# Background steps that start at granule 12 of a feed-forward layer, and two GpSimd splits in place of six

## The chip, the cores and the metric

The kernel runs on one core of one Trainium2 chip. The metric is the device time of one execution, in microseconds (us), as the median of several runs. The engines are named as the profile names them: PE is TensorE, DVE is VectorE, ACT is ScalarE, POOL is GpSimd, and SP is SyncE, whose queue issues nearly all weight loads.

## The reference, cut to what matters

Two blocks are computed on one sequence of 256 rows of 1024 numbers. The first has two layers; each is a feed-forward layer (FFN1), a token mixer, a gated projection (ple) and a second feed-forward layer (FFN2), with a layer norm after FFN1, after the mixer and after FFN2. The second block is a hybrid mixer and a mixture of experts. Its inputs are modulated by a vector that hangs on `c` alone and not on the sequence:

```python
def swiglu(x, w_up, w_down):
    a, b = jnp.split(x @ w_up, 2, axis=-1)
    return (jax.nn.silu(a) * b) @ w_down

# first block, for i in range(2)
x = layer_norm(ALPHA * x + 0.5 * swiglu(x, ffn1_up[i], ffn1_down[i]), ln1_g[i], ln1_b[i])
mix = token_mix(x, ...)
x = layer_norm(ALPHA * x + mix, ln2_g[i], ln2_b[i])
ple = jax.nn.sigmoid(x @ w_ple_gate[i]) * (p[i] @ w_ple[i])
x = layer_norm(ALPHA * x + 0.5 * swiglu(x, ffn2_up[i], ffn2_down[i]) + ple, ln3_g[i], ln3_b[i])

# second block
cond = jax.nn.silu(c)
mod = cond @ w_ada[layer] + b_ada[layer]          # 1024 -> 6144
sh_m, sc_m, g_m, sh_f, sc_f, g_f = jnp.split(mod, 6, axis=-1)
```

All is float32. `D_FF` is 2816, so the up matrix has 5632 columns.

## The kernel before, in words

**Matmuls of split numbers.** A float32 weight matrix is loaded in granules of 128 x 1024 numbers (512 KB, `raw`). `load_split` (L227) takes each granule: SP issues the load (L237), ACT writes the rounded high part (`whi`, L161), and DVE or POOL writes the rest (`wlo`, L165). `products` (L211) then makes three matmuls from each pair: high by high (L223), low by high (L224), high by low (L225). A granule is worth 12 matmuls of 512 columns, six for each half `t` of the sequence. There are four `raw` buffers, seven pairs of `whi` and `wlo`, and four pairs more in a pool that lives for one feed-forward layer.

**A feed-forward layer** (`ffn`, L312 before the change) runs over six chunks of the up matrix, five of 512 columns and one of 256, each with an `a` part and a `b` part: 44 granules. Then come the 22 granules of the down matrix. In the first chunk `gemms` (L197) does all eight granules for t=0 and then all eight for t=1, so PE wants a new granule after every six matmuls; in the later chunks it does both halves of a granule in turn. The tuples `pl1` and `pl2` name the granules of the first chunk's `a` and `b` part whose `wlo` is made on POOL: (2, 3) and (0, 1, 2, 3) before. They count for FFN2 of the first layer and both feed-forward layers of the second. `done_b` has DVE multiply `th` by the `b` part (L329) and PE transpose the product (`tp`, L251), which becomes `hh` and `hl`, the input of the down part. The down part ends with its last eight granules for t=0, then the layer norm of t=0 on DVE (L284 to L293) while PE does the same granules for t=1, then the layer norm of t=1; each norm ends with PE transposing `x` (L251) for what follows.

**Background work.** The modulation needs no result of the sequence, and is done in pieces during the feed-forward layers: rows 0 to 3 of the twelve rows of 512 numbers in FFN1 of the first layer (after a list of other constants), rows 4 to 7 in FFN2 of the first layer, rows 8 to 11 in FFN1 of the second. `ada` is a generator; a row has eight steps, each a load of 256 KB (`araw`, two buffers, L833) and a DVE instruction that adds it into `acc` (L842). A finished row is split, summed by two PE matmuls with ones (L820, L821) and written to memory. `load_split` calls `background(1)` once per granule, which runs the generator to its next `yield`. Before, every second step yields twice, so 32 steps take 48 granules.

**What sets the order.** The program is written in the order of the calls, and a scheduler then orders each engine's instructions by priority and by when their inputs come free. An instruction may so be put far ahead of the place where it was written. `pin` (L111) keeps an instruction in program order. Each engine works through its queue strictly in order, and SP too.

Of the kernel before, what the change touches and what calls it, by code (L numbers as in the profile page):

```python
# [14 lines left out]
OP = mybir.AluOpType  # L15
# [56 lines left out]
class Kernel:  # L72
    def __init__(self, tc, a, out, dbg=None):
        self.tc, self.nc, self.a, self.out, self.dbg = tc, tc.nc, a, out, dbg
        self.n = 0
        self.nraw, self.nhl, self.next, self.xp = 4, 7, 4, None
        self.npj, self.ngt, self.glag = 4, 4, 1
        self.dtail = 8
        self.xg = 4
        self.sp, self.late = None, False  # L80
        self.pre, self.npre = [], 5
        self.start = False
        self.na, self.nb = 8, 9
        self.pl1, self.pl2 = (2, 3), (0, 1, 2, 3)
        self.bg = iter(())
        self.scr = {"s4": (1024, 8), "s2": (512, 6)}


# [216 lines left out]
        self.xp = None  # L305

    def background(self, n):
        for _ in range(n):
            next(self.bg, None)

# [499 lines left out]
    def ada(self, r0, r1):  # L810

        nc = self.nc
        w, b = self.a["w_ada_2"][0], self.a["b_ada_2"][0]
        with self.tc.tile_pool(name=self.nm("ada"), bufs=1, side="right") as pool:
            def finish(i, acc):
                hl = self.st(self.wp, [P, 1024], "whi", F32R, bufs=self.nhl)
                hi, lo = hl[:, :512], hl[:, 512:]
                self.split_from(acc, hi, lo)
                pb = self.ps("tp")
                nc.tensor.matmul(pb, self.ones, hi, start=True, stop=False)  # L820
                nc.tensor.matmul(pb, self.ones, lo, start=False, stop=True)  # L821
                nc.scalar.activation(acc[0:1, :], pb[0:1, :], AF.Copy, bias=1.0 if i // 2 in (1, 4) else 0.0)
                nc.gpsimd.dma_start(self.mod[i // 2:i // 2 + 1, (i % 2) * 512:(i % 2) * 512 + 512], acc[0:1, :])

            def start(i):
                acc = self.st(pool, [P, 512], "acc", bufs=2)
                nc.vector.memset(acc, 0.0)
                nc.sync.dma_start(acc[0:1, :], b[i * 512:(i + 1) * 512].rearrange("(o n) -> o n", o=1))
                return acc

            def load(j):
                raw = self.st(pool, [P, 512], "araw", bufs=2)
                nc.sync.dma_start(raw, self.wsrc(w, j % KD, 1, j // KD * 512, 512)[:, 0, :])  # L833
                return raw

            nxt, last, ahead = start(r0), None, load(r0 * KD)
            for i in range(r0, r1):
                acc = nxt
                for k in range(KD):
                    raw, j = ahead, i * KD + k + 1  # L840
                    ahead = load(j) if j < r1 * KD else None
                    nc.vector.scalar_tensor_tensor(acc, raw, self.cond[:, k:k + 1], acc, op0=OP.mult, op1=OP.add)  # L842
                    if k == 3 and last:
                        finish(*last)
                    if k == 5 and i < r1 - 1:
                        nxt = start(i + 1)
                    yield
                    if j % 2:
                        yield
                last = i, acc  # L850
            yield
            finish(*last)
# [980 lines left out]
    def run(self):  # L1833
        nc, a, tc = self.nc, self.a, self.tc
        with tc.tile_pool(name="const", bufs=1) as self.cp, tc.tile_pool(name="small", bufs=2) as self.smp, \
# [23 lines left out]
            with tc.tile_pool(name="ln", bufs=1) as self.lnp:  # L1859
                pl, self.pl1, self.pl2 = (self.pl1, self.pl2), (), ()  # L1860
                for L in range(2):
                    ln = a["ln1_g"][L], a["ln1_b"][L]
                    if L:
                        self.pl1, self.pl2 = pl
                    if L:
                        self.bg = self.ada(8, 12)
                    self.ffn(a["ffn1_up"][L], a["ffn1_down"][L], ln)
                    self.background(999)
                    if self.stop(f"ln1_{L}"):
                        return  # L1870
                    ln = a["ln2_g"][L], a["ln2_b"][L]
                    self.token_mix(L, ln)
                    if self.stop(f"ln2_{L}"):
                        return
                    self.ple(L)
                    self.pl1, self.pl2 = pl
                    ln = a["ln3_g"][L], a["ln3_b"][L]
                    if L == 0:
                        self.bg = self.ada(4, 8)
                    else:  # L1880
                        self.mods = ctx.enter_context(tc.tile_pool(name="mods", bufs=1, side="right"))
                        A, sh = self.mod_pair(self.mods, 0, a["norm_mix_2"][0])
                    self.ffn(a["ffn2_up"][L], a["ffn2_down"][L], ln, last=(load_first, norm_first) if L else None)
                    self.background(999)
                    if self.stop(f"ln3_{L}"):
                        return
# [49 lines left out]
```

## Time and profile before

| what | us |
| --- | --- |
| median of 3 runs | 2527.62 (2524.69 to 2527.79) |
| the profiled execution, whole | 2525.59 |
| its span, first to last instruction | 2524.0 |
| PE busy in the span | 2389.5 (95%) |
| DVE busy | 1313.9 (52%) |
| ACT busy | 827.1 (33%) |
| POOL busy | 209.1 (8%) |

The first block takes about 1310 us. In it FFN1 of the first layer lies at 0 to 216, its FFN2 at about 464 to 671, FFN1 of the second layer at 671 to 872, and its FFN2 at about 1117 to 1310. What follows 1330 us (the mixture of experts, above all) is bound by weight loads, and no line of the change stands in it. In the rows, the number after a `x` counts instructions, a bracket says how long the engine was idle before the first of them, and the name behind `<-` in the bracket is what ended the idle time.

### The profile page before, as it was taken

To read this page: it belongs to the slowest core of one execution; us is meant where nothing else is said; L and a number is where in the kernel's file an instruction comes from. 1 tells how busy PE (TensorE), PEld (TensorE's weight loads), DVE (VectorE), ACT (ScalarE), POOL (GpSimd) and SP (SyncE) were. 2 spreads that over 40 slices of the span, in tenths; PEclk is the share of its full clock that TensorE was granted. 3 is DMA by queue.
4 is the path that set the end of the run, shared out by engine and by line. 5 is a ranking of instruction groups with operands and counts; after the bars stand their busy time and mean duration, and the time that the engine had idled before them with its cause. 6 is when DMAs were issued, how large, how long until landed. Compare 5 with 4: busy or idle time off the path is not lost.

```text
span 2524.0 us, 29376 instructions
## 1 busy us (share of the span) xinstructions
PE 2389.5 (95%) x11078; PEld 1562.4 (62%) x11078; DVE 1313.9 (52%) x2243; ACT 827.1 (33%) x1227; POOL 209.1 (8%) x191
## 2 busy tenths in 40 slices
PE   8998999999799999999988999999999999999998
PEld 6887787778678878878877877433333333333332
DVE  7768757666666676675566775322222222222222
ACT  5443544444345454444435753100000001000000
POOL 4000211200200011230013010000000000000000
PEclk9999999999899999999998999999999999999999
DMA  8777465567666656566547467999999999999997
GB/s 272 242 236 233 144 188 182 184 215 222 210 188 215 217 159 175 171 197 195 184 131 232 118 199 289 399 421 421 420 421 421 420 421 420 420 421 421 421 421 325
DMA packets 202027, 705.94 MB, mean 280 GB/s; under 512 B 18122, under 2 KB 31642, under 8 KB 152984
## 3 DMA queue, kind: packets, MB, share of 16 engines
q1 hardware_dynamic: 194584, 684.02, 74.1%
q0 software_dynamic: 7296, 19.99, 2.7%
q8 instruction: 89, 1.46, 0.2%
q14 instruction: 58, 0.48, 0.1%
HBM read 702.83 MB, written 3.47 MB: 280 GB/s over the span
## 4 chain that ended last, share of the span: by engine, by line
PE 53%; DMA 31%; DVE 9%; issue 3%; ACT 3%; POOL 1%; SPq 0%; ACTq 0%; DVEq 0%; POOLq 0%
DMA mraw<-in_w_dram 25%; PE mm L225 12%; PE mm L224 12%; PE mm L223 12%; PE mm L1590 5%; PE sc L1621 4%; PE tp L251 3%; DVE wlo L165 2%; DMA araw<-in_w_ada_dram 2%; DMA raw<-in_ffn_up_dram 2%; ACT whi L161 1%; DMA raw<-in_w_in_dram 1%; PE tp L1700 1%; PE sc L1519 1%; DVE x L292 1%
## 5 line engine op out<-in xcount | busy, mean ns | idle before, releaser
L165 DVE TENSOR_TENSOR wlo<-raw,whi 128x1024 fp32r<-128x1024 f32 (+1 forms) x451 | 559.0, 1246 | 277.2 <-ACT whi L161 274.5
L161 ACT ACTIVATE whi<-raw 128x1024 fp32r<-128x1024 f32 x478 | 500.7, 1055 | 521.5 <-PE mm L225 386.3
L224 PE MATMUL mm<-wlo,xTh 128*128 128x512 f32 (+2 forms) x1520 | 580.4, 382 | 10.6 <-POOL wlo L165 8.6
L223 PE MATMUL mm<-whi,xTh 128*128 128x512 f32 (+2 forms) x1520 | 585.8, 386 | 2.1 <-ACT whi L161 1.7
L225 PE MATMUL mm<-whi,xTl 128*128 128x512 f32 (+2 forms) x1520 | 579.8, 382 | 0.0
L1590 PE MATMUL mm<-mraw,xe 128*64 128x512 f32 x1920 | 488.5, 613 | 33.6 <-DMA mraw<-in_w_dram 33.5
L1590 PEld LDWEIGHTS mm<-mraw,xe 128*64 128x64 f32 x1920 | 150.6, 141 | 332.6 <-issue 265.2
L224 PEld LDWEIGHTS mm<-wlo,xTh 128*128 128x128 f32 x1520 | 288.6, 190 | 69.8 <-POOL wlo L165 11.5
L223 PEld LDWEIGHTS mm<-whi,xTh 128*128 128x128 f32 x1520 | 289.0, 190 | 56.2 <-ACT whi L161 3.0
L225 PEld LDWEIGHTS mm<-whi,xTl 128*128 128x128 f32 x1520 | 288.6, 190 | 50.0
L1601 ACT ACTIVATE mt<-mg 128x256 f32<-128x256 f32 x64 | 26.6, 416 | 691.5 <-DVE mg L1600 689.5
L1621 PE MATMUL sc<-mraw,xTl 128*64 128x512 f32 x976 | 231.5, 597 | 7.4 <-ACT xe L1530 7.4
L1600 DVE TENSOR_SCALAR mg<-mm 128x256 f32<-128x256 f32 x64 | 27.2, 424 | 323.4 <-PE mm L1590 319.0
L1621 PEld LDWEIGHTS sc<-mraw,xTl 128*64 128x64 f32 x976 | 69.1, 137 | 125.6 <-issue 108.9
L225 PE MATMUL mm<-whi,hl 128*128 128x512 f32 x352 | 138.1, 392 | 0.0
L223 PE MATMUL mm<-whi,hh 128*128 128x512 f32 x352 | 137.6, 391 | 0.0
L224 PE MATMUL mm<-wlo,hh 128*128 128x512 f32 x352 | 137.5, 391 | 0.0
L1626 DVE TENSOR_TENSOR xTh<-sc,gf 128x512 f32<-128x512 f32 x32 | 22.1, 692 | 208.4 <-PE sc L1621 208.4
L1701 DVE TENSOR_TENSOR x<-x,tp 128x512 f32<-128x512 f32 x68 | 46.8, 688 | 129.8 <-PE tp L1700 129.8
L842 DVE SCALAR_TENSOR_TENSOR acc<-araw,cond,acc 128x512 f32<-128x512 f32 x96 | 72.8, 758 | 54.2 <-DMA araw<-in_w_ada_dram 51.8
L165 POOL TENSOR_TENSOR wlo<-raw,whi 128x1024 fp32r<-128x1024 f32 x27 | 68.9, 2564 | 285.6 <-ACT whi L161 285.5
L225 PEld LDWEIGHTS mm<-whi,hl 128*128 128x128 f32 x352 | 66.4, 189 | 13.6
(445 smaller groups left out, 2277.5 us busy)
## 6 DMA issues: line engine op xcount, KB each, us to landing
mraw<-in_w_dram SPq DMA_DIRECT2D x360, 1024.0 KB, 19.8
raw<-in_ffn_up_dram SPq DMA_DIRECT2D x176, 512.0 KB, 4.4
raw<-in_w_in_dram SPq DMA_DIRECT2D x142, 512.0 KB, 4.4
raw<-in_ffn_down_dram SPq DMA_DIRECT2D x88, 512.0 KB, 4.0
araw<-in_w_ada_dram SPq DMA_DIRECT2D x96, 256.0 KB, 3.6
AS<-in_w_dram SPq DMA_DIRECT2D x22, 1024.0 KB
raw<-in_w_branch_dram SPq DMA_DIRECT2D x28, 512.0 KB, 3.9
raw<-in_w_out_dram SPq DMA_DIRECT2D x16, 512.0 KB, 3.7
```

Of the source, the lines that this page charges most:

```text
L161: ins = self.nc.scalar.activation(hi, src, AF.Copy)
L165: ins = (self.nc.gpsimd if pool else self.nc.vector).tensor_tensor(lo, src, hi, op=OP.subtract)
L223: nc.tensor.matmul(banks[b], xh, hi[:, s], start=kc == 0, stop=False)
L224: nc.tensor.matmul(banks[b], xh, lo[:, s], start=False, stop=False)
L225: nc.tensor.matmul(banks[b], xl, hi[:, s], start=False, stop=kc == nk - 1)
L251: self.nc.tensor.transpose(pt[:s.shape[-1], i * P:i * P + s.shape[0]], s, self.ident)
L842: nc.vector.scalar_tensor_tensor(acc, raw, self.cond[:, k:k + 1], acc, op0=OP.mult, op1=OP.add)
L1590: self.pe(nc.tensor.matmul(ph[nb][e * 64:e * 64 + 64], xe[:, k, e * 64:e * 64 + 64], units[e][k][:, nb * 512:nb * 512 + 512], start=False, ...
L1600: nc.vector.tensor_scalar(g, pv[:, :, 0], 7.0, None, op0=OP.min)
L1601: nc.scalar.activation(th, g, AF.Tanh, scale=0.851)
L1621: self.pe(self.nc.tensor.matmul(py[c][e * 64:e * 64 + 64], aT[:, k:k + 64], units[e][j][:, o:o + 512], start=j == 0 and r == 0, stop=j == ...
L1701: nc.vector.tensor_tensor(self.x[t][:, s], self.x[t][:, s], po, op=OP.add)
```

## The change

Four things are done at once.

1. A counter `hold` is set to 12 when the generators for rows 4 to 7 and 8 to 11 are set up. The first twelve calls of `background(1)` of that layer only count it down.
2. The double `yield` goes, so there is one step per granule, and one `yield` comes after a generator's first loads. A generator of 32 steps takes 34 granules: 12 to 45 of the 66 in the two layers with `hold`, and 34 in place of 49 behind the constants in the first.
3. The first DVE step of each generator is pinned to its place in the program.
4. `pl1`, `pl2` become (), (1, 3): two `wlo` of the first chunk on POOL in place of six, in three feed-forward layers. DVE has 12 instructions more in all and POOL 12 fewer.

```diff
-        self.pl1, self.pl2 = (2, 3), (0, 1, 2, 3)
-        self.bg = iter(())
+        self.pl1, self.pl2 = (), (1, 3)
+        self.bg, self.hold = iter(()), 0
...
     def background(self, n):
+        if n == 1 and self.hold:
+            self.hold -= 1
+            return
         for _ in range(n):
             next(self.bg, None)
...
             nxt, last, ahead = start(r0), None, load(r0 * KD)
+            yield
             for i in range(r0, r1):
...
-                    nc.vector.scalar_tensor_tensor(acc, raw, self.cond[:, k:k + 1], acc, op0=OP.mult, op1=OP.add)
+                    ins = nc.vector.scalar_tensor_tensor(acc, raw, self.cond[:, k:k + 1], acc, op0=OP.mult, op1=OP.add)
+                    if (i, k) == (r0, 0):
+                        self.pin(ins)
...
                     yield
-                    if j % 2:
-                        yield
...
-                        self.bg = self.ada(8, 12)
+                        self.bg, self.hold = self.ada(8, 12), 12
...
-                        self.bg = self.ada(4, 8)
+                        self.bg, self.hold = self.ada(4, 8), 12
```

**The layer norm that ends FFN2 of the first layer, on DVE** (`x_71` is half t=0; `wlo_57..` are splits for the coming FFN1; L842 is a step of the modulation). Before:

```order
L165 TENSOR_TENSOR wlo_5350<-raw_5347,whi_5349 128x1024
L165 TENSOR_TENSOR wlo_5722<-raw_5719,whi_5721 128x1024
L284 SCALAR_TENSOR_TENSOR x_71<-mm_5353,x_71 128x512
L285 BN_STATS bn_1201_5573<-x_71 128x6
L842 SCALAR_TENSOR_TENSOR acc_5925<-araw_6014,cond,acc_5925 128x512
L842 SCALAR_TENSOR_TENSOR acc_5925<-araw_6029,cond,acc_5925 128x512
L284 SCALAR_TENSOR_TENSOR x_71<-mm_5354,x_71 128x512
L842 SCALAR_TENSOR_TENSOR acc_5925<-araw_6038,cond,acc_5925 128x512
L285 BN_STATS bn_1201_5573<-x_71 128x6
L842 SCALAR_TENSOR_TENSOR acc_5925<-araw_6123,cond,acc_5925 128x512
L287 BN_AGGR mv_1202_5578<-bn_1201_5573 128x2
```

And with the change:

```order
L165 TENSOR_TENSOR wlo_5728<-raw_5725,whi_5727 128x1024
L165 TENSOR_TENSOR wlo_5734<-raw_5731,whi_5733 128x1024
L284 SCALAR_TENSOR_TENSOR x_71<-mm_5353,x_71 128x512
L285 BN_STATS bn_1201_5573<-x_71 128x6
L284 SCALAR_TENSOR_TENSOR x_71<-mm_5354,x_71 128x512
L285 BN_STATS bn_1201_5573<-x_71 128x6
L287 BN_AGGR mv_1202_5578<-bn_1201_5573 128x2
```

Sixteen steps of rows 8 to 11 stood in and before this norm, ahead of the layer that they were written in, seven of them from its first L285 on; now none does. The same holds for rows 4 to 7 and the norm that ends FFN1 of the first layer.

**The norm of t=1 (`x_72`) behind it, on DVE, with the change.** The splits that have left POOL, and the first `th` of FFN1, stand inside the chain of the norm:

```order
L285 BN_STATS bn_1212_5664<-x_72 128x6 x2
L165 TENSOR_TENSOR wlo_5748<-raw_5745,whi_5747 128x1024
L287 BN_AGGR mv_1213_5669<-bn_1212_5664 128x2
L165 TENSOR_TENSOR wlo_5760<-raw_5757,whi_5759 128x1024
L142 TENSOR_SCALAR rv_1214_5671<-mv_1213_5669 128x1
L292 SCALAR_TENSOR_TENSOR x_72<-x_72,mv_1213_5669,lng_5207 128x512
...
L328 SCALAR_TENSOR_TENSOR th_5795<-th_5795,mm_5743 128x512
...
L165 TENSOR_TENSOR wlo_5896<-raw_5893,whi_5895 128x1024
L156 SCALAR_TENSOR_TENSOR ry_1216_5675<-rt_1218_5679,ry_1216_5675 128x1
L293 SCALAR_TENSOR_TENSOR x_72<-x_72,ry_1216_5675,lnb_5208 128x512 x2
```

On PE, 42 matmuls of FFN1's t=0 half now stand between the end of the down part and the transposes of `x_72`.

**The start of FFN2 of the first layer, on DVE** (L788, L789 before and L791, L792 after are the end of ple). Before, and with the change:

```order
L165 TENSOR_TENSOR wlo_4064<-raw_4061,whi_4063 128x1024
L788 SCALAR_TENSOR_TENSOR pg_3990<-pg_3990,pe_844_3882 128x512
L789 SCALAR_TENSOR_TENSOR x_71<-pg_3990,x_71 128x512
L165 TENSOR_TENSOR wlo_4081<-raw_4078,whi_4080 128x1024
L788 SCALAR_TENSOR_TENSOR pg_4018<-pg_4018,pe_838_3860 128x512
L789 SCALAR_TENSOR_TENSOR x_72<-pg_4018,x_72 128x512
L788 SCALAR_TENSOR_TENSOR pg_4046<-pg_4046,pe_845_3884 128x512
L789 SCALAR_TENSOR_TENSOR x_72<-pg_4046,x_72 128x512
L325 SCALAR_TENSOR_TENSOR th_4160<-th_4160,mm_4102 128x512
```

```order
L165 TENSOR_TENSOR wlo_4070<-raw_4067,whi_4069 128x1024
L791 SCALAR_TENSOR_TENSOR pg_4018<-pg_4018,pe_838_3860 128x512
L165 TENSOR_TENSOR wlo_4076<-raw_4073,whi_4075 128x1024
L792 SCALAR_TENSOR_TENSOR x_72<-pg_4018,x_72 128x512
L165 TENSOR_TENSOR wlo_4082<-raw_4079,whi_4081 128x1024
L791 SCALAR_TENSOR_TENSOR pg_4046<-pg_4046,pe_845_3884 128x512
L792 SCALAR_TENSOR_TENSOR x_72<-pg_4046,x_72 128x512
L165 TENSOR_TENSOR wlo_4090<-raw_4087,whi_4089 128x1024
L165 TENSOR_TENSOR wlo_4102<-raw_4099,whi_4101 128x1024
L328 SCALAR_TENSOR_TENSOR th_4137<-th_4137,mm_4085 128x512
```

DVE takes the splits of `a` 2, `a` 3, `b` 0 and `b` 2 between the steps of ple; POOL keeps `b` 1 and `b` 3.

## Rows read from the trace of the kernel before

**Rows 1.** The page: busy time of the engines in the whole span

```profile
PE 2389.5 (95%) x11078; PEld 1562.4 (62%) x11078; DVE 1313.9 (52%) x2243; ACT 827.1 (33%) x1227; POOL 209.1 (8%) x191
```

**Rows 2.** Who PE waited for, whole span: us in total, times, longest

```profile
PE tp L251 <- DVE x L293: 25.0, 7, 8.1
PE tp L251 <- DVE th L329: 5.6, 4, 3.0
```

**Rows 3.** Busy time by stretch: length, PE PEld DVE ACT POOL, clock, DMA

```profile
147.60:272.39 124.79, 116.88 (x526) 94.32 (x525) 91.80 (x173) 54.77 (x79) 7.82 (x11) 0.96 0.70 220
810.29:924.94 114.65, 113.26 (x525) 91.90 (x524) 75.93 (x146) 53.50 (x77) 8.26 (x12) 1.00 0.61 194
600.05:671.49 71.44, 63.32 (x279) 51.99 (x278) 45.13 (x62) 26.50 (x29) 6.76 (x5) 0.95 0.69 222
810.29:872.41 62.12, 61.90 (x278) 50.75 (x278) 36.58 (x48) 26.97 (x30) 3.96 (x7) 1.00 0.68 222
671.49:693.57 22.08, 15.73 (x62) 12.69 (x61) 18.76 (x26) 7.77 (x10) 10.50 (x6) 0.85 0.64 198
```

**Rows 4.** Timeline of PE: the transposes of x at three norms

```profile
216.64 1.94 PE L251 MATMUL tp<-ident,x 128*128 128x128 f32 x8 [7.21 <-DVE x L293]
665.95 1.09 PE L251 MATMUL tp<-ident,x 128*128 128x128 f32 x4 [8.12 <-DVE x L293]
683.89 1.09 PE L251 MATMUL tp<-ident,x 128*128 128x128 f32 x4 [6.35 <-DVE x L293]
```

**Rows 5.** Timeline of DVE, inside the norm of t=0 at 654 us

```profile
653.79 2.60 DVE L842 SCALAR_TENSOR_TENSOR acc<-araw,cond,acc 128x512 f32<-128x512 f32 x2 [7.09 <-DMA araw<-in_w_ada_dram]
```

**Rows 6.** Who PE waited for at 465:485 us; the answer for 1120:1135 reads alike

```profile
PE mm L224 <- POOL wlo L165: 3.9, 3, 1.6
```

**Rows 7.** Timeline of POOL, DVE and ACT at the start of FFN2, first layer

```profile
461.20 8.20 POOL L165 TENSOR_TENSOR wlo<-raw,whi 128x1024 fp32r<-128x1024 f32 x3 [13.88 <-ACT whi L161]
459.11 0.69 DVE L789 SCALAR_TENSOR_TENSOR x<-pg,x 128x512 f32<-128x512 f32 x1
461.57 2.77 DVE L789 SCALAR_TENSOR_TENSOR x<-pg,x 128x512 f32<-128x512 f32 x1
474.40 2.52 DVE L165 TENSOR_TENSOR wlo<-raw,whi 128x1024 fp32r<-128x1024 f32 x1 [0.26 <-ACT whi L161]
478.35 1.87 DVE L165 TENSOR_TENSOR wlo<-raw,whi 128x1024 fp32r<-128x1024 f32 x1 [1.43 <-ACT whi L161]
469.98 2.95 ACT L161 ACTIVATE whi<-raw 128x1024 fp32r<-128x1024 f32 x3 [3.42 <-DVE x L789]
```

**Rows 8.** Timeline of PE, two matmuls that follow each other at 476 us

```profile
476.46 0.39 PE L223 MATMUL mm<-whi,xTh 128*128 128x512 f32 x1
476.69 0.40 PE L224 MATMUL mm<-wlo,xTh 128*128 128x512 f32 x1
```

**Rows 9.** Timeline of DVE, the undisturbed norm of t=1, first and last piece

```profile
872.46 1.28 DVE L284 SCALAR_TENSOR_TENSOR x<-mm,x 128x512 f32<-128x512 f32 x2
...
878.25 1.42 DVE L293 SCALAR_TENSOR_TENSOR x<-x,ry,lnb 128x512 f32<-128x512 f32 x2
```

**Rows 10.** Timeline of PE: transposes of th that came late

```profile
44.61 0.66 PE L251 MATMUL tp<-ident,th 128*128 128x128 f32 x4 [1.13 <-DVE th L329]
540.60 0.66 PE L251 MATMUL tp<-ident,th 128*128 128x128 f32 x4 [3.00 <-DVE th L329]
750.84 0.66 PE L251 MATMUL tp<-ident,th 128*128 128x128 f32 x4 [1.33 <-DVE th L329]
```

**Rows 11.** Timeline of DVE, the step ahead of the second of these

```profile
539.19 0.75 DVE L842 SCALAR_TENSOR_TENSOR acc<-araw,cond,acc 128x512 f32<-128x512 f32 x1 [4.67 <-DMA araw<-in_w_ada_dram]
```

**Rows 12.** One chunk of FFN2, first layer: length, DVE busy, clock, DMA, GB/s

```profile
565.17:587.92 22.75, 17.12 (x21) 1.00 0.72 222
```

**Rows 13.** Groups of DVE instructions in that chunk: busy, mean ns, idle before

```profile
L165 DVE TENSOR_TENSOR wlo<-raw,whi 128x1024 fp32r<-128x1024 f32 x7 | 8.5, 1220 | 2.1 <-ACT whi L161 2.1
L842 DVE SCALAR_TENSOR_TENSOR acc<-araw,cond,acc 128x512 f32<-128x512 f32 x7 | 5.2, 748 | 3.3 <-DMA araw<-in_w_ada_dram 3.3
```

## The prediction

> **What bounds the kernel now.** I read the page first. PE is busy 95% of the span and no other engine over 52% [rows 1], so time can come only from PE's idle stretches and from stretches in which PE's clock is granted at half. The list of PE's waits names them: 25.0 us behind the last step of a layer norm (`x`, L293), 5.6 us behind `th` of a chunk (L329) [rows 2], and twice 3.9 us behind splits on POOL at the start of the two FFN2 [rows 6]. What lies after 1330 us waits for weights and is not touched by the change, so a microsecond saved before it should be a microsecond at the end.
>
> Then I compare stretches that do the same work. From the first down matmul of FFN1 to the same transposes in the mixer takes 124.79 us in the first layer and 114.65 in the second, the first two of [rows 3], with 526 and 525 PE instructions. From the first down matmul of FFN2, first layer, to the first matmul of the next layer takes 71.44 us, against 62.12 for the same part of FFN1, second layer, the next two of [rows 3], with 279 and 278. In the slower of each pair PE waits 7.21 and 8.12 us for a norm [rows 4], and the granted clock is 0.96 and 0.95 against 1.00. Why the norm is late is seen on DVE: there stands a modulation step that idles the engine for 7.09 us until its load lands [rows 5], with the norm queued behind it.
>
> **The change part by part.** The sum is made against the profiled execution, 2525.59 us; the median of the runs shown is 2.0 us above it.
>
> *Steps out of the norm that ends FFN1, first layer.* The pinned first step keeps all of rows 4 to 7 in FFN2. DVE's order there becomes that of the second layer, which has its own measurement: 124.79 - 114.65 = **10.1 us** gained. The two retired PE sums of a finished row move elsewhere in the same program and cost the same.
>
> *Steps out of the norm that ends FFN2, first layer.* Likewise, 71.44 - 62.12 = **9.3 us**.
>
> *Start of both FFN2, POOL's six splits become two.* PE uses up a granule every six matmuls, 6 x 0.23 = 1.4 us [rows 8]. POOL takes 8.20 / 3 = 2.7 us for a split, DVE 1.22 [rows 7, 13]. Six on POOL are 16 us for eight granules that PE wants within 11; that is the 3.9 us [rows 6]. Now POOL has two (5.4 us) and DVE six (7.3 us), side by side, both under 11. DVE also gets its other work back faster: L789 takes 0.69 us alone and 2.77 while POOL splits, and three `whi` on ACT wait 3.42 us for it [rows 7]. Bounds: nothing, if the splits now wait on DVE as long as they did on POOL, and the whole 3.9. I take the whole, as DVE's row is below PE's pace: 2 x 3.9 = **7.8 us**.
>
> *Start of FFN1, second layer.* Here PE waits 6.35 us for the norm of t=1 [rows 4], in a stretch at clock 0.85, the last of [rows 3]. Undisturbed, the chain from the first L284 to the first half of L293 takes 878.25 + 0.7 - 872.46 = 6.5 us [rows 9]. The change puts three splits (3 x 1.22 = 3.7) and a `th` (0.7) into it: 10.9. Two of the splits meet POOL's two; such a split took 2.52 and 1.87 in place of 1.22 [rows 7], together 2.0 more: 12.9. PE now has 42 matmuls to do meanwhile, 42 x 0.23 = 9.7. It would still wait 12.9 - 9.7 = 3.2 us in place of 6.35, a gain of **3.2 us**. I count nothing for the clock.
> By the Trainium skill (SBUF — State Buffer, section "Who interferes with whom") a DVE instruction with two SBUF inputs and a GpSimd instruction that reads SBUF exclude each other, and whoever is late waits for the whole of the other. By that rule each split could wait a whole POOL split of 2.7 us, the chain would be 6.5 + 3.7 + 0.7 + 5.4 = 16.3 us, and nothing would be gained here; the rows (a delay of 1.3 and 0.65) are of splits that came when POOL's was partly done. With no meeting at all, the chain is 10.9 and the gain 5.2. So 0 and 5 are the ends.
>
> *Steps into the up parts.* Before, 64 of the 96 steps ran in up or down parts without harming a norm, and PE lost 1.13 + 3.00 + 1.33 = 5.5 us to them [rows 10]: a `th` came late because a step ahead of it waited for its load, 4.67 us in the worst case [rows 11]. Now 96 steps run there. At the same rate they cost 5.5 x 96 / 64 = 8.2 us, **2.7 us** more. Is there room on DVE? A chunk of the changed order has eight steps and eight splits. The chunk at 565 us had seven and seven, was 17.12 us busy of 22.75, waited 3.3 us for loads [rows 12, 13], and PE had no idle row in it. With one more of each, 17.1 + 0.75 + 1.22 = 19.1 us, which leaves 3.6 us for waits where 3.3 were seen. It fits, just. Bounds: all the loss goes (5.5 gained), or each chunk loses 3.0 (below).
>
> *The loads.* SP's queue has the modulation's loads in other places, none new. Two `araw` and two `acc` loads per generator still go early, in the down part of the layer before; two buffers are all there are, so no more can, and no step on DVE waits behind them there. The 14.6 us of splits that DVE takes from POOL (12 x 1.22) are counted above, where they stand; elsewhere DVE's idle time covers them.
>
> Sum: 10.1 + 9.3 + 7.8 + 3.2 - 2.7 = 27.7 us. 2525.59 - 27.7 = 2497.9 for an execution like the profiled one, and 2499.9 by the median. I forecast **2499 us**.
>
> **The rivals.**
>
> *A: DVE and its loads become the bound of the up parts, and the kernel is slower.* Some twelve chunks (four in each of three layers) now carry steps at nearly every granule, and SP must fetch each `araw` between weight loads, with two buffers. If in each chunk one load lands as late as the one at 539 us and PE waits 3.0 us behind it [rows 10, 11], that is 36 us, 30.5 more than now, which eats up all the other terms (30.4): 2525.7. At the 4.67 us that DVE waited, 56 us, 50.5 more: 2545.7. It decides from 3.0 us per chunk on. For it: only 3.6 us are free in a chunk. Against it: with seven steps a chunk ran without a PE gap, and the mean loss before was 5.5 us over nine chunks, 0.6 each. Chance 0.07.
>
> *B: splits on DVE are as late as on POOL.* Then the starts give nothing: 10.1 + 9.3 - 2.7 = 16.7, 2508.9. If moreover PE waits for each of the 12 moved splits, 14.6 us go: 2523.5. For it: DVE has ple and the norm to do at these places. Against it: 1.22 against PE's 1.4 us. The Trainium skill (Perfetto Trace Analysis, section "Optimizing Scalar/DVE Operations") says that offloading to GpSimd may make sense where DVE is saturated; by that the change goes the wrong way here, though the same sentence warns of the shared port. Chance 0.15.
>
> *C: the steps still run ahead.* If the pin held the first step only in name, the norms would stay late and only 7.8 + 3.2 = 11.0 be gained: 2514.6. The order of the changed program speaks against it. Chance 0.03.
>
> *D: more goes.* The second norm's wait vanishes whole (6.35) and the up parts lose nothing: 10.1 + 9.3 + 7.8 + 6.4 + 5.5 = 39.1: 2486.5. Chance 0.12.
>
> **How the numbers follow.** 0.63 is left for the forecast, whose own range is 2492 to 2507. The range reaches from a little below D to just beyond C, 2485 to 2516, and leaves out A and the costly end of B. A measurement of this kernel can tell some 0.2%, 5 us, from no change. Slower is A but for its lower end, 0.06; within 0.2% are that end and the costly end of B, 0.03; faster is the rest, 0.91.
>
> **What would show it.** PE's waits behind L293 at the norms of FFN1 and FFN2, first layer, should be under 1 us, and the stretches of the first two pairs read about 115 and 62 us, at clock 1.00. PE's waits for POOL at the two FFN2 should be gone, with L789's successor at 0.7 us. At the start of FFN1, second layer, a wait of about 3 us should stay. PE's waits behind `th` should sum to some 8 us; 30 or more would mean A. DVE should show 12 more splits of 128x1024 and POOL 12 fewer. The prediction is wrong if the norms stay late although no step stands in them, or if DVE waits for `araw` longer than the 3.6 us that a chunk leaves free.

## The result, and the profile after

The changed kernel takes **2501.13 us** (median of 4 runs, 2499.63 to 2504.71), against 2527.51 us for the kernel before on the same chip (4 runs, 2524.69 to 2527.79): a ratio of 0.990, 95% interval 0.9887 to 0.9914. The forecast was 2499 us, and the range 2485 to 2516. The profiled execution took 2501.3 us, its span 2499.5, 24.5 less than the span before. Line numbers of the changed kernel are three or four higher from `background` on: L332 is the old L329, L792 the old L789, L836 the old L833, L846 the old L842.

The page of the changed kernel, busy time of the engines:

```profile
PE 2385.3 (95%) x11078; PEld 1560.2 (62%) x11078; DVE 1311.6 (52%) x2255; ACT 828.2 (33%) x1227; POOL 178.6 (7%) x179
```

DVE has 12 instructions more and POOL 12 fewer [rows 1]. PE does the same work; the gain is in what it waits for and in its clock. Who PE waited for, whole span (total, times, longest):

```profile
PE tp L251 <- DVE th L332: 11.7, 9, 3.4
PE tp L251 <- DVE x L293: 5.8, 6, 2.1
...
PE mm L224 <- POOL wlo L165: 1.9, 1, 1.9
```

The 25.0 us behind `x` [rows 2] have become 5.8, and the 3.9 us at each FFN2 start [rows 6] are gone from those stretches. The 5.6 us behind `th` have doubled. The same by stretch, changed kernel; the first three lines answer to the first, third and last of [rows 3], the last two are the up parts of FFN2 (first layer) and FFN1 (second layer), from the first transposes of `th` to the first down matmul:

```profile
150.88:265.04 114.16, 113.11 (x525) 92.01 (x524) 77.27 (x148) 54.14 (x77) 7.16 (x10) 1.00 0.63 194
592.22:654.28 62.06, 61.92 (x278) 50.86 (x278) 36.24 (x48) 27.87 (x30) 2.03 (x3) 1.00 0.61 195
654.28:669.96 15.68, 13.57 (x65) 10.99 (x64) 15.50 (x28) 7.01 (x9) 5.29 (x4) 1.00 0.66 213
471.15:592.22 121.07, 116.87 (x570) 97.94 (x571) 90.05 (x109) 54.85 (x67) 1.51 (x3) 0.99 0.75 238
669.96:792.16 122.20, 117.94 (x570) 98.66 (x569) 89.77 (x109) 54.85 (x67) 2.66 (x5) 0.97 0.74 235
```

The two up parts in the kernel before:

```profile
481.60:600.06 118.46, 115.46 (x573) 96.69 (x571) 79.67 (x93) 55.31 (x67) 1.51 (x3) 1.00 0.68 215
693.57:810.29 116.72, 115.39 (x573) 96.68 (x571) 78.64 (x92) 55.33 (x67) 2.67 (x5) 1.00 0.66 205
```

The norm stretches now read 114.16 and 62.06, within 0.5 us of their counterparts in the second layer, at clock 1.00. The up parts have sixteen DVE instructions more each (x109 for x93 and x92): they are the steps that stood in the norms. They are 2.6 and 5.5 us longer. In these two layers, and in FFN2 of the second, the first transposes of `th` come three matmuls later than before (x570 for x573), so 0.7 us of work counts in the start that was counted in the up part; their sum is not touched by it.

**The start of FFN1, second layer.** DVE's timeline in the changed kernel, from the first L284 of the t=1 norm to its L293:

```profile
653.80 1.37 DVE L284 SCALAR_TENSOR_TENSOR x<-mm,x 128x512 f32<-128x512 f32 x2 [2.32 <-PE mm L225]
...
656.28 3.25 DVE L165 TENSOR_TENSOR wlo<-raw,whi 128x1024 fp32r<-128x1024 f32 x1
...
659.57 1.17 DVE L165 TENSOR_TENSOR wlo<-raw,whi 128x1024 fp32r<-128x1024 f32 x1
...
665.18 1.41 DVE L293 SCALAR_TENSOR_TENSOR x<-x,ry,lnb 128x512 f32<-128x512 f32 x2
```

POOL's two splits at that time, and PE's transposes of `x` behind the norm:

```profile
653.68 4.77 POOL L165 TENSOR_TENSOR wlo<-raw,whi 128x1024 fp32r<-128x1024 f32 x2 [53.35 <-ACT whi L161]
```

```profile
666.08 0.63 PE L251 MATMUL tp<-ident,x 128*128 128x128 f32 x4 [2.11 <-DVE x L293]
```

One DVE split takes 3.25 us where the next takes 1.17; it stands beside POOL's second split. The chain is 665.18 + 0.7 - 653.80 = 12.1 us, and PE waits 2.11 us in place of 6.35 [rows 4].

**How a `th` comes late.** The longest wait of the changed kernel, 3.37 us at 706 us, in the second layer's FFN1. DVE:

```profile
698.54 0.75 DVE L846 SCALAR_TENSOR_TENSOR acc<-araw,cond,acc 128x512 f32<-128x512 f32 x1 [0.22 <-DMA araw<-in_w_ada_dram]
...
703.60 0.75 DVE L846 SCALAR_TENSOR_TENSOR acc<-araw,cond,acc 128x512 f32<-128x512 f32 x1 [1.38 <-DMA araw<-in_w_ada_dram]
704.27 1.22 DVE L165 TENSOR_TENSOR wlo<-raw,whi 128x1024 fp32r<-128x1024 f32 x1
705.41 1.27 DVE L332 TENSOR_TENSOR th<-th,mm 128x512 f32<-128x512 f32 x2
```

SP, which issues the loads, and then PE:

```profile
699.32 0.33 SPq L836 DMA_DIRECT2D araw<-in_w_ada_dram  x1
```

```profile
706.14 1.12 PE L251 MATMUL tp<-ident,th 128*128 128x128 f32 x4 [3.37 <-DVE th L332]
...
709.62 0.63 PE L223 MATMUL mm<-whi,xTh 128*128 128x512 f32 x1
710.05 0.63 PE L224 MATMUL mm<-wlo,xTh 128*128 128x512 f32 x1
```

With two `araw` buffers a load can go out only when the step two before it has read its buffer: the step of 698.54 ends at 699.29 and SP issues at 699.32. The step that needs the load runs at 703.60, after DVE has idled 1.38 us; a split and `th` are queued behind it, and PE behind `th`. The cost does not end there. After the wait PE's matmuls follow each other at 0.43 us in place of 0.23 [rows 8], and the granted clock says why (changed kernel, 708 to 712 us):

```profile
708.00:712.00 4.00, 4.00 (x12) 3.23 (x11) 3.18 (x5) 0.60 (x1) 0.00 (x0) 0.50 0.85 279
```

PE is busy without a gap there, at the lower of its two levels, 1.2 GHz. The length of a wait does not tell by itself whether the clock falls behind it. Behind a wait of 2.6 us at 507 us it was 0.66, behind the 2.11 us wait at 666 us it stayed at 1.00 (both in the changed kernel), and so it did behind the wait of 3.00 us in the kernel before [rows 10]:

```profile
508.00:512.00 4.00, 4.00 (x14) 3.30 (x14) 3.27 (x5) 0.85 (x3) 0.00 (x0) 0.66 1.02 379
668.00:672.00 4.00, 4.00 (x21) 3.31 (x20) 3.59 (x5) 2.70 (x5) 0.00 (x0) 1.00 0.88 267
540.60:544.00 3.40, 3.40 (x19) 2.70 (x20) 3.40 (x5) 1.20 (x2) 0.00 (x0) 1.00 0.55 146
```

**Where the steps stand.** The chunk whose `th` is 3.37 us late (from the transposes of `th` at 680.8 to those at 706.1) holds ten steps on DVE, and so does the same chunk of FFN2, first layer (482.2 to 506.7), whose `th` is 2.6 us late; the three chunks that follow in each layer hold four, five and eight. What DVE waited for loads in these two, FFN2 first:

```profile
DVE acc L846 <- DMA araw<-in_w_ada_dram: 7.0, 6, 1.8
DVE acc L846 <- DMA araw<-in_w_ada_dram: 7.7, 7, 2.0
```

The prediction named waits of more than 3.6 us in a chunk as a sign that it is wrong; here that sign came.

### The profile page after: what moved, and what is told of

Read it like the earlier page. It is cut to its first block, busy times and chain, and to the rows that moved or that the text cites. A ratio compares the mean times of both kernels' runs of the same rounds, so it can differ in the third digit from the quotient of the medians.

```text
span 2499.5 us, 29387 instructions
## 1 busy us (share of the span) xinstructions
PE 2385.3 (95%) x11078; PEld 1560.2 (62%) x11078; DVE 1311.6 (52%) x2255; ACT 828.2 (33%) x1227; POOL 178.6 (7%) x179
## 4 chain that ended last, share of the span: by engine, by line
PE 41%; DMA 33%; DVE 8%; issue 3%; ACT 2%; POOL 0%; SPq 0%; DVEq 0%; ACTq 0%; POOLq 0%
DMA mraw<-in_w_dram 28%; PE mm L224 10%; PE mm L225 10%; PE mm L223 10%; PE mm L1594 4%; PE sc L1625 3%; DMA araw<-in_w_ada_dram 3%; DVE wlo L165 2%; PE tp L251 2%; ACT whi L161 1%; PE tp L1704 1%; DMA raw<-in_ffn_up_dram 1%; DVE acc L846 1%; DMA raw<-in_w_in_dram 0%; DMA acc<-in_b_ada_dram 0%
## 5 line engine op out<-in xcount | busy, mean ns | idle before, releaser
L165 DVE TENSOR_TENSOR wlo<-raw,whi 128x1024 fp32r<-128x1024 f32 (+1 forms) x463 | 575.1, 1249 | 271.2 <-ACT whi L161 269.3
L1630 DVE TENSOR_TENSOR xTh<-sc,gf 128x512 f32<-128x512 f32 x32 | 22.1, 692 | 208.4 <-PE sc L1625 208.4
L846 DVE SCALAR_TENSOR_TENSOR acc<-araw,cond,acc 128x512 f32<-128x512 f32 x96 | 71.8, 748 | 41.1 <-DMA araw<-in_w_ada_dram 35.4
L224 PEld LDWEIGHTS mm<-wlo,hh 128*128 128x128 f32 x352 | 66.1, 188 | 13.5
```

The lines of the kernel that those rows point to most:

```text
L165: ins = (self.nc.gpsimd if pool else self.nc.vector).tensor_tensor(lo, src, hi, op=OP.subtract)
L224: nc.tensor.matmul(banks[b], xh, lo[:, s], start=False, stop=False)
L846: ins = nc.vector.scalar_tensor_tensor(acc, raw, self.cond[:, k:k + 1], acc, op0=OP.mult, op1=OP.add)
```

## The experiments

The theory: the up parts lose time because steps wait for loads that two buffers let out too late, not because there are more steps. The rival: DVE has too much to do there. Beside this, each part of the change was tried alone. All numbers of a run stand in one table. The ratio is to the runs of before on the same chip. The kernel before took 2527.5 to 2529.5 us on the chips used, so kernels of different chips are compared by their ratios, and a forecast that is 2 us away from a time is not missed by that alone. The stretches are read from PE's timeline of the profiled execution: the norm parts run from the first down matmul to the first matmul of what follows (FFN1 and FFN2 of the first layer), "start" is the start of FFN1, second layer, as in the last line of [rows 3], and the up parts are those of FFN1 and FFN2, first layer, and FFN1, second, the first of them from the kernel's first matmul on. "th" is what PE waited for `th`, "araw" what DVE waited for the steps' loads, both over the whole span.

| kernel | us | ratio (95%) | norm parts | start | up parts | th | araw |
| --- | --- | --- | --- | --- | --- | --- | --- |
| before | 2527.51 | 1 | 70.8, 71.4 | 22.1 | 136.9, 118.5, 116.7 | 5.6 | 51.8 |
| the change | 2501.13 | 0.990 (0.9887-0.9914) | 62.0, 62.1 | 15.7 | 140.6, 121.1, 122.2 | 11.7 | 35.4 |
| only_pool | 2513.99 | 0.9936 (0.9919-0.9952) | 69.0, 70.3 | 19.9 | 136.7, 119.1, 116.0 | 4.9 | 47.7 |
| only_steps | 2518.71 | 0.9949 (0.9931-0.9967) | 62.0, 64.2 | 20.5 | 140.6, 122.0, 119.7 | 12.3 | 36.3 |
| no_pin | 2516.82 | 0.9957 (0.9943-0.9971) | 69.7, 70.6 | 17.2 | 139.3, 115.6, 116.9 | 4.0 | 45.4 |
| hold0 | 2503.72 | 0.9922 (0.9897-0.9947) | 62.0, 67.3 | 18.6 | 137.6, 117.2, 117.5 | 3.9 | 31.2 |
| hold22 | 2500.09 | 0.9878 (0.9861-0.9894) | 62.0, 63.5 | 15.7 | 138.8, 119.1, 118.3 | 8.8 | 42.8 |
| thin | 2499.47 | 0.9884 (0.9867-0.9900) | 63.3, 64.7 | 17.3 | 137.3, 119.3, 117.9 | 7.0 | 47.1 |
| araw3 | 2494.28 | 0.9871 (0.9854-0.9887) | 62.0, 62.1 | 15.7 | 136.7, 116.5, 122.3 | 7.2 | 15.7 |
| araw4 | 2492.97 | 0.9849 (0.9832-0.9865) | 62.0, 62.1 | 15.7 | 138.4, 116.4, 116.8 | 3.3 | 7.1 |
| araw5 | 2487.23 | 0.9843 (0.9827-0.9860) | 62.0, 62.1 | 15.7 | 138.2, 115.9, 116.7 | 2.5 | 3.2 |
| araw4_pool0 | 2493.40 | 0.9862 (0.9845-0.9878) | 62.0, 62.1 | 19.6 | 136.7, 117.5, 117.2 | 3.7 | 9.4 |
| old_araw4 | 2517.34 | 0.9958 (0.9945-0.9970) | 63.4, 72.1 | 20.0 | 137.0, 116.0, 116.9 | 2.2 | 17.6 |

How far a stretch varies by itself can be read in the first up part: the change, only_steps, hold0, no_pin and hold22 have the same order of steps and splits on DVE there, and it reads 140.6, 140.6, 137.6, 139.3 and 138.8. The four kernels with the old spacing (before, only_pool, thin, old_araw4) have 25 steps there in place of 32 and read 136.7 to 137.3. What follows the first block, where no step stands, reads 1209.7 to 1214.3 in the 13 traces.

### The two halves of the change

The kernel before with the new tuples, and nothing else:

```diff
-        self.pl1, self.pl2 = (2, 3), (0, 1, 2, 3)
+        self.pl1, self.pl2 = (), (1, 3)
```

> The kernel before with the two new tuples alone (two splits on POOL in place of six), steps as before. If the terms of the trace add up, the starts of both FFN2 give 8.4 us (4.1 and 4.3 were read from the changed kernel), and the start of FFN1, second layer, gives 3 to 6 us more, since POOL's splits no longer slow the norm of t=1: 2512 to 2517 us. Rival: the gain at the start of FFN1 came from the steps that had left, not from POOL: 2519 us. PE's waits of 7.2 and 8.1 us for the norms stay in both cases.

Measured: 0.64% faster. There is no wait for POOL at either FFN2 start, and from the first layer's norm to the first `th` of FFN2 it took 258.83 us in place of 263.18, in the second layer 257.67 in place of 261.92: 4.3 us each. The norms stay late (PE waited 5.58 and 6.97 us at them, 7.21 and 8.12 before [rows 4]). The start of FFN1, second layer, gave 2.2 us and not the 3 to 6 that were expected.

The change with the old tuples, so that counter, spacing and pin stand alone:

```diff
-        self.pl1, self.pl2 = (), (1, 3)
+        self.pl1, self.pl2 = (2, 3), (0, 1, 2, 3)
```

> The change without the new tuples: hold, one step per granule and the pin, with six splits on POOL as before. The norms give 10.6 + 9.4 us, the up parts cost 12.0 (all read from the changed kernel), the starts give nothing: a gain of about 8, so 2517 to 2520 us, and with the run of the tuples alone it should add up to the whole gain of 26 us. Rival: the two parts help each other (the splits on POOL make DVE late in the up parts too): over 2522 us here.

Measured: 0.51% faster. Who PE waited for:

```profile
PE tp L251 <- DVE x L293: 12.4, 7, 4.8
PE tp L251 <- DVE th L332: 12.3, 7, 3.1
PE mm L224 <- POOL wlo L165: 8.3, 7, 1.6
```

The first norm is free and the second all but 2.4 us of its wait (64.2 in place of 62.1), the POOL waits stay, and the late `th` come with the steps and not with the splits that DVE takes over. The two halves make 0.9936 x 0.9949 = 0.9885, against 0.990 for both at once, which these intervals do not tell apart. At the start of FFN1, second layer, they do not simply add up: 2.2 us by the tuples alone, 1.6 by the steps alone, 6.4 by both.

### Pin and counter

The change without the pin:

```diff
-                    if (i, k) == (r0, 0):
-                        self.pin(ins)
```

> The change with the pin of a generator's first step left out; the counter of 12, one step per granule and the new tuples stay. In the order of DVE, sixteen steps of rows 4 to 7 and sixteen of rows 8 to 11 then stand in and around the two norms of the first layer again. If it is the pin that freed the norms, PE's waits behind x (L293) come back there (7 us or more each at the norms ending FFN1 and FFN2 of the first layer), the two norm stretches are 8 to 10 us longer each, the up parts lose some 4 to 6 us less since fewer steps stand there, and the time is 2511 to 2518 us. If the norms were freed by the counter and the thinner steps alone, the time stays at 2501.

Measured: 2516.82, inside what the theory of the pin gave; the profiled execution, which the stretches show, was the fastest of the five at 2508.04, so the stretches account for 7 us of the loss, and where the other four executions (2516 to 2519) lost some 8 to 11 us more is in no trace. The waits are back at both norms, and a step with its wait stands between the pieces of the norm (PE's timeline, then DVE's):

```profile
217.55 1.73 PE L251 MATMUL tp<-ident,x 128*128 128x128 f32 x7 [7.09 <-DVE x L293]
...
659.37 1.94 PE L251 MATMUL tp<-ident,x 128*128 128x128 f32 x8 [6.25 <-DVE x L293]
```

```profile
205.58 0.75 DVE L846 SCALAR_TENSOR_TENSOR acc<-araw,cond,acc 128x512 f32<-128x512 f32 x1 [1.46 <-DMA araw<-in_w_ada_dram]
206.24 0.69 DVE L285 BATCH_NORM_STATS2 bn<-x 128x6 f32<-128x512 f32 x1
```

Though they are written twelve granules later, the steps still ran ahead of their layer; the pin is what ties them to it.

The change with the counter at 0:

```diff
-                        self.bg, self.hold = self.ada(8, 12), 12
+                        self.bg, self.hold = self.ada(8, 12), 0
...
-                        self.bg, self.hold = self.ada(4, 8), 12
+                        self.bg, self.hold = self.ada(4, 8), 0
```

> The change with the counter at 0 in both layers; pin, one step per granule and new tuples stay. The steps of rows 4 to 7 and 8 to 11 then begin with the first chunk, eleven to sixteen granules sooner; on DVE the first four steps of rows 8 to 11 stand between the two norms that end FFN2 of the first layer and the next four between the t=1 norm and the first th. If the counter is needed beside the pin, the start of FFN1, second layer, loses its 6 us again and the start of FFN2, first layer, some 2 to 4, and the time is 2506 to 2512 us. If the pin alone does the work, the time stays at 2500 to 2502; it could gain a little from fewer steps in the later chunks.

Measured: 2503.72, between the two, and by its interval not told apart from the change. The stretches say why so little shows. At the end of FFN2 the first pinned step stands on DVE just ahead of the first L284 of the t=0 norm. There it waits for its load (DVE), three more steps inside the norm wait another 3.0 us, and PE waits for the norm:

```profile
634.25 0.75 DVE L846 SCALAR_TENSOR_TENSOR acc<-araw,cond,acc 128x512 f32<-128x512 f32 x1 [2.30 <-DMA araw<-in_w_ada_dram]
```

```profile
649.31 1.09 PE L251 MATMUL tp<-ident,x 128*128 128x128 f32 x4 [3.40 <-DVE x L293]
```

The norm part costs 5.3 us more, the start 3.0, and the start of FFN2, first layer, 3.0 too (261.20 in place of 258.25 from the norm on); the two later up parts give back 3.9 and 4.8, and the first read 3.0 less. With two buffers the counter moves the loss more than it removes it.

### Fewer and later steps

The counter at 22 in place of 12, in both layers:

```diff
-                        self.bg, self.hold = self.ada(8, 12), 12
+                        self.bg, self.hold = self.ada(8, 12), 22
...
-                        self.bg, self.hold = self.ada(4, 8), 12
+                        self.bg, self.hold = self.ada(4, 8), 22
```

> The changed kernel with a hold of 22 granules in place of 12 in both layers: the first step stands behind granule 23, and the last ten or so of a layer in the down part, where no th is made and DVE has one split of 1.22 us per 2.7 us of PE. By theory 2 (too many DVE instructions ahead of th) a third of the steps no longer delays a th, and the up parts lose 3 to 5 us less: 2495 to 2499 us. By theory 1 (late loads) the late th only moves to a later chunk: 2499 to 2502. Rival: the last steps run into the norm and bring its wait back: over 2505.

And the second yield of every second step put back (`thin`), so that 32 steps take 48 granules:

```diff
                     yield
+                    if j % 2:
+                        yield
```

> The change with the second yield of every second step put back, so that 32 steps take 48 granules, 12 to 60 of the 66, with counter, pin and new tuples as changed. If the up parts lose time because a step at every granule asks for its load sooner than two buffers let it come, thinner steps meet loads that have landed: the DVE waits for araw (35.4 us in the change) fall below 20, the waits of PE behind th fall from 11.7 to some 5, and the time is 2494 to 2498 us. If the up parts lose by the number of steps on DVE, about as many th come late and the time stays at 2500 to 2502; if the later steps reach the down part's end and delay a norm, it is 2503 or more.

Neither is told apart from the change: 2500.09 and 2499.47. `hold22` does not decide between its two theories: its time lies in the range of the late loads, but its ratio puts it at 0.9878 x 2527.51 = 2496.7 us on the chip of the change, in the range of too many instructions. Eight steps of each layer ran on into the stretch behind the up part, and the norm parts of FFN2, first layer, and FFN1, second, read 63.5 and 64.1 in place of 62.1 and 62.0. In `thin` one expectation failed outright: DVE's waits for `araw` did not fall below 20 us but rose.

```profile
DVE acc L846 <- DMA araw<-in_w_ada_dram: 47.1, 45, 2.5
```

Of 96 steps 45 wait in place of 39. But on DVE the steps are not sparser where it counts: the scheduler still put ten of them into the chunk of FFN2 that ends with a late `th` (479.6 to 505.1 us), and there DVE waited as before:

```profile
DVE acc L846 <- DMA araw<-in_w_ada_dram: 7.9, 7, 2.1
```

So `thin` does not show what truly spread steps would do. The late `th` did fall, from 11.7 us to 7.0, and the two later up parts are 1.8 and 4.3 us shorter, but the norm parts are 1.3 and 2.6 longer, that of FFN1, second layer, 2.1, and the start 1.6. Part of that is work that has only moved: the down part of FFN2 holds 280 PE instructions in place of 278. Writing the steps further apart is no cure by itself.

### More buffers for the loads

The change with more `araw` buffers; `araw3` and `araw5` have 3 and 5 in the same place:

```diff
-                raw = self.st(pool, [P, 512], "araw", bufs=2)
+                raw = self.st(pool, [P, 512], "araw", bufs=4)
```

> The changed kernel with four buffers for the modulation's loads in place of two. Theory 1: the up parts lose 12 us because a step waits on DVE for its load (35 us of waits) and th is queued behind it; with four buffers the loads land earlier, the waits for araw fall below 12 us and the up parts lose 4 us: 2491 to 2495 us. Theory 2: DVE simply has too many instructions ahead of th, one step to each split, and waits only in time that it had; then the waits fall as well and the time stays at 2499 to 2503 us.

> The change with three araw buffers in place of two. In the change a load is asked for one granule (2.8 us) before its step and takes 3.0 us to land, so one granule more of lead should do: if the lead is the matter, the time is 2493 to 2495 us and the araw waits of DVE fall from 35.4 us to under 12. If it goes by the number of loads that can pile up, it is half way, 2496 to 2498.

> The change with five araw buffers. With four the araw waits of DVE were 7.1 us and the th waits of PE 3.3. If the lead of a load is the matter, four were enough and the time stays at 2492 to 2494 us. If more loads ahead still help, 2489 to 2491. If the modulation's loads, asked for sooner, push weight loads back on SP, 2495 or more.

Each buffer takes some of the waits away, and five leave nearly none. DVE's waits for `araw` with four, then with five buffers:

```profile
DVE acc L846 <- DMA araw<-in_w_ada_dram: 7.1, 10, 1.4
```

```profile
DVE acc L846 <- DMA araw<-in_w_ada_dram: 3.2, 3, 1.9
```

The two later up parts with five buffers:

```profile
467.67:583.53 115.86, 115.37 (x570) 96.50 (x571) 90.05 (x109) 54.89 (x68) 1.51 (x3) 1.00 0.75 243
661.32:777.99 116.67, 114.93 (x571) 96.31 (x569) 90.02 (x109) 54.76 (x67) 3.15 (x5) 1.00 0.74 240
```

DVE has as many instructions there and is as long busy as in the change (90.05 and 90.02 us, there 90.05 and 89.77), and the stretches are 5.2 and 5.5 us shorter, at clock 1.00. The chunks that held ten steps and waited 7.0 and 7.7 us hold eleven now and wait 1.2 and 1.9, and PE does not wait for their `th`. That settles it against the number of steps, and the fall of the waits speaks for the loads. The order of DVE changed with the buffers (the chunk behind those holds no step in place of four), and how much of the gain hangs on the order was not tried apart. Three buffers were enough for FFN2 (116.5) and not for the second layer's FFN1 (122.3), where one `th` was still 4.25 us late: the sum of DVE's waits does not tell which of them lies ahead of a `th`. With 15.7 us they also stayed above the 12 that were expected. Four and five buffers are not told apart by their intervals, but both are faster than either kernel: `araw5` at 2487.23 is the fastest that was run, and faster than all three of its forecasts. Its traced execution is 7.3 us shorter than that of `araw4`, but 4.2 of them lie behind the first block, so the fifth buffer is not shown to help.

The same four buffers on the kernel before:

> The kernel before with four araw buffers and nothing else. With four buffers the scheduler itself leaves no step of rows 4 to 7 in the norm that ends FFN1 of the first layer; sixteen steps of rows 8 to 11 still stand in and around the norm that ends FFN2. If a step harms a norm by its late load and not by its own 0.75 us, both norm stretches come to within 3 us of 114 and 62 us, and the time is 2505 to 2511 us, with the POOL waits of the starts and the late t=1 norm left. If the steps harm it by standing there, the second norm stretch stays at about 70 us and the time is 2514 to 2518. If two buffers cost nothing in the old order, 2527.

Measured: 2517.34. The scheduler's order freed the first norm (63.4), and the second stayed late, at 72.1. That came out as the theory of "standing there" had it, but the trace shows that the late load counts for more. DVE, inside the norm that ends FFN2, between its first L285 and its second L284:

```profile
645.75 4.60 DVE L842 SCALAR_TENSOR_TENSOR acc<-araw,cond,acc 128x512 f32<-128x512 f32 x4 [6.95 <-DMA araw<-in_w_ada_dram]
650.27 0.68 DVE L284 SCALAR_TENSOR_TENSOR x<-mm,x 128x512 f32<-128x512 f32 x1
```

DVE idles 6.95 us for a load, then takes 4.60 us over four steps, and the norm's second L284 stands behind all of it. Why the load is late is seen on SP:

```profile
628.59 12.95 SPq L237 DMA_DIRECT2D raw<-in_ffn_up_dram  x7
641.59 11.63 SPq L833 DMA_DIRECT2D araw<-in_w_ada_dram  x10
```

Seven weight loads of the next layer stand ahead of it in the queue, and each waited for DVE to free a buffer, 9.2 us in all. In the kernel before it is the same: seven such loads from 636.49 us on, and the step's load behind them from 648.50. More `araw` buffers do not help a load that is asked for that late; only the order takes it out of the norm.

### The last two splits off POOL

The change with four buffers and `pl2` empty:

```diff
-        self.pl1, self.pl2 = (), (1, 3)
+        self.pl1, self.pl2 = (), ()
```

> The change with four araw buffers, and with the last two first-chunk splits taken off POOL too (pl2 empty). If POOL's two splits still hold up DVE at the start of FFN1, second layer, PE's wait of 2 us there goes and the time is 2490 to 2492 us, against 2493 with four buffers alone. If DVE cannot keep eight splits in time beside ple and the norm, PE waits for wlo from DVE at the three starts, 2 us or more each, and the time is 2496 to 2500. If neither counts, 2493.

Measured: 2493.40, no different from four buffers alone, but not for lack of effect. The start of FFN1, second layer, went from 15.7 to 19.6 us, the opposite of the first expectation. DVE's chain of the t=1 norm and PE behind it:

```profile
645.86 1.37 DVE L284 SCALAR_TENSOR_TENSOR x<-mm,x 128x512 f32<-128x512 f32 x2 [2.32 <-PE mm L225]
...
661.38 1.41 DVE L293 SCALAR_TENSOR_TENSOR x<-x,ry,lnb 128x512 f32<-128x512 f32 x2
```

```profile
662.27 1.94 PE L251 MATMUL tp<-ident,x 128*128 128x128 f32 x8 [4.89 <-DVE x L293]
```

No split is held up now, but more of them stand in the chain, which takes 661.38 + 0.7 - 645.86 = 16.2 us in place of 12.1; PE waits 4.89 us in place of 2.11. What paid for it elsewhere is not settled: the first up part is 1.7 us shorter, and what follows the first block 3.6, both within what these stretches vary from run to run. For this start, two splits on POOL are right.

## Why the prediction was right, and where not

The sum was 27.7 us and the span fell by 24.5. Term by term, from the two traces:

| term | forecast | measured |
| --- | --- | --- |
| norm that ends FFN1 | 10.1 | 124.79 - 114.16 = 10.6 |
| norm that ends FFN2 | 9.3 | 71.44 - 62.06 = 9.4 |
| start of both FFN2 | 7.8 | 3.1 + 4.3 = 7.4 |
| start of FFN1, second layer | 3.2 | 22.08 - 15.68 = 6.4 |
| steps into the up parts | -2.7 | -3.7 - 2.6 - 5.5 = -11.8 |
| all the rest | 0 | 2.5 |
| sum | 27.7 | 24.5 |

The 3.1 us at FFN2, first layer, are what is left when 0.8 us that the mixer ahead of it lost are taken off. Of the 2.5 in "all the rest", 1.3 lie behind the first block, within what that part varies by itself: luck.

**The two norms** were right, and for the reason given: comparing a stretch with its twin that does the same work undisturbed gave 10.1 and 9.3 without a model. `no_pin` shows that the steps in the norm are the cause, and that rival C was one line away.

**The start of FFN2** was right: the POOL waits are gone there, and L792 takes 0.69 us in place of 2.77 [rows 7]. DVE's timeline, changed kernel:

```profile
452.65 0.69 DVE L792 SCALAR_TENSOR_TENSOR x<-pg,x 128x512 f32<-128x512 f32 x1
...
456.14 0.68 DVE L792 SCALAR_TENSOR_TENSOR x<-pg,x 128x512 f32<-128x512 f32 x1
```

Rival B fell with it. Of the Trainium skill's advice (Perfetto Trace Analysis, section "Optimizing Scalar/DVE Operations") to offload where DVE is saturated, the runs bear out the condition: with DVE at 52% of the span, taking splits off POOL gained 0.64%; where DVE's chain sets PE's wait, as at the start of FFN1, the two left on POOL are worth 4.89 - 2.11 = 2.8 us of PE's wait. The prediction took that advice to speak against the change; its condition was not met here, so it does not (and the page's warning of the shared port is its next sentence, not the same one).

**The start of FFN1, second layer,** was right in kind and half in size. The step "Two of the splits meet POOL's two" was too dear by one: one met, and was 3.25 - 1.22 = 2.0 us longer, the chain 12.1 and not 12.9, and the wait 2.11 and not 3.2. And "I count nothing for the clock" left out 2.2 us: PE was busy for 13.57 us in place of 15.73 for the same kind of work, at 1.00 in place of 0.85. The rule of the Trainium skill (SBUF — State Buffer, section "Who interferes with whom") that a late DVE split waits for the whole of POOL's instruction agrees with that one split, which came about 0.2 us into POOL's second (4.77 / 2 = 2.4 us each); the count of meetings, not the rule, decided that there was a gain.

**The step that failed** is "At the same rate they cost 5.5 x 96 / 64 = 8.2 us", 2.7 more; 11.8 were lost. Three things are wrong in it. First, the rate was averaged over three layers, but the up part of the first went only from 25 steps to 32, and the two others from 16 to 32: at the same rate their loss of 3.0 + 1.3 us [rows 10] would have doubled. All waits behind `th` came to 11.7 us, 6.1 more than before, and not to 8.2. Second, a wait was priced by its own length, as if PE took up at full speed behind it. PE was busy for 0.5, 1.4 and 2.6 us more in the three up parts, and behind the 3.37 us wait the clock stood at 0.50. These two make 6.1 + 4.5 = 10.6 of the 11.8 us. Third, "It fits, just" counted on eight steps in a chunk and 3.3 us of waits. The chunks with the two longest waits of PE have ten steps and 7.0 and 7.7 us. Not the room on DVE was short but the lead of a load: with five buffers eleven steps stand there and `th` comes in time. Some of the 3.7 us in the first up part is no effect at all: five kernels with the same order read 137.6 to 140.6 there, on average 2.4 us above the four with the old spacing.

Rival A was thus the right mechanism at two fifths of its price (11.8 us in place of 30.5). That the forecast came out close is in part luck: 3.2 us of unplanned gain at the start of FFN1 and 2.5 elsewhere hid most of the 9.1 us by which this term missed. The bound from above (all the loss goes) is what the versions with four and five buffers come near to: 3.3 and 2.5 us behind `th`.

## What to carry to other kernels

Background work does harm less by running than by waiting: a step of 0.75 us with a late load holds up everything queued behind it on its engine. So ask first when its load may go out: two buffers tie it to the step two before, and an earlier load in the same queue that waits for its own buffer holds it up too. Two more buffers of 256 KB brought half as much again as the whole change (a ratio of 0.985 in place of 0.990). Where an order is left to a scheduler, tie down the first instruction of a group, and read the clock behind a wait of PE before the wait is priced.

## What was not expected

Steps written further apart waited more for their loads (47.1 us in 45 waits, against 35.4 in 39). The scheduler left them as dense where they began; why later ones waited more too is open. A buffer count alone moved sixteen steps out of the first norm, since the scheduler's order hangs on it. And taking the last splits off POOL, with which no split on DVE was held up any more at the start of FFN1, made that start 3.9 us slower.
